# Turning picked heads on GpSimd, adding bias and sinks on TensorE, and another order where a mixer takes over

## The chip, the cores and the metric

The kernel runs on one core of one Trainium2 chip. The metric is device microseconds of one execution; less is better. Engines are called by their names: TensorE multiplies matrices (PE, and PEld for its weight loads), VectorE (DVE), ScalarE (ACT) and GpSimd (POOL) work element by element, SyncE (SP) issues DMAs.

## The reference

A decoder trunk of two layers works on 256 tokens of width 1024, everything in fp32. Each layer is a mixer and a squared-ReLU MLP, each between a modulation and a LayerNorm:

```python
for layer in range(DEPTH):
    shift, scale, gate = ada_modulation(c, ada_w[layer, 0], ada_b[layer, 0])   # silu(c) @ w + b
    h = x * (1.0 + scale) + shift
    y = mixer_ab(h, ...) if layer % 2 == 0 else mixer_c(h, ...)
    x = layer_norm(DN_ALPHA * x + gate * y, ln_g[layer, 0], ln_b[layer, 0])
    ...                                       # the same again with the MLP in place of the mixer
```

`mixer_ab` of layer 0 has two groups of eight heads. Group A attends in a window of 128 tokens, and each head has a learned sink, a logit that takes part in the softmax but has no value. Group B scores all keys with a small indexer, picks the 64 best for each query and attends to these; its queries are `apply_rope(cq @ w_uq)`, those of the indexer `apply_rope(cq @ w_uiq)`. The rotary embedding is

```python
t1, t2 = jnp.split(t, 2, axis=-1)
rot = jnp.concatenate([-t2, t1], axis=-1)
return t * cos + rot * sin
```

`mixer_c` of layer 1 has sixteen heads with rotary queries and keys and plain causal attention (there is one block of 256 keys only).

## The kernel before

The 256 tokens are two blocks b of 128, one token to a partition. Products that need fp32's precision at a higher rate are split: a weight w is copied by ScalarE to wh (line 182), VectorE subtracts to get wl (line 183, for `w_out` GpSimd does it), and `mm3` adds three fp32r products (lines 263 to 265, tiles ps_m, ps_c, ps_out). The first attention runs on plain fp32 matmuls.

A scheduler orders each engine's instructions from the program's order, priorities (`later(n)` moves a piece back) and added dependencies without a semaphore (`behind(what, m)` places m after the last instruction noted under that name). What an engine then runs is a fixed list, and an instruction that waits holds up all behind it on its engine. PSUM tiles come from four pools a to d of two buffers each: ps_ada and ps_uq are in a, ps_s (scores) and ps_i (index scores) in b, transposes (ps_T, ps_pt, ps_mod) in c, ps_pv in d.

**The first attention** (about 50 to 100 us). `b_queries` multiplies the queries of group B (which = 0) or of the indexer (1) into ps_uq (line 819), `rope` turns them on VectorE (lines 503 to 507: one product with the cosine, one half product each with the two halves of the sine, one sum), `to_T` transposes (line 523) and ScalarE copies to bqT or iqT (line 525). `iq(0)`, `iq(1)`, `bq(0)`, `bq(1)` are written before the attention, bq with a lower priority. `index` computes index scores (ps_i; relu at line 854 on ScalarE; the weighted sum at line 857 on VectorE), `select` picks eight at a time (lines 868, 869 and at the end 873).

`attend` runs four half steps for each block and group (`half_step`, a pipeline of three stages): scores on TensorE (line 564), mask and minimum on VectorE (line 568), exp on ScalarE (line 572), transposes (line 578), and products with the values into ps_pv (line 586), whose 65th column of each head is the sum. Behind every second half step VectorE forms the denominator: for group A the sink term (`sinkexp`, line 595, from negm and the constant nsink, both in SBUF; exp at line 596; line 597 adds), reciprocal (598), and the scaled output y (602).

Beside each half step `ada_rows` multiplies a piece of the conditioning weights (eight matmuls of 128x256, line 378, tile ps_ada), ScalarE copies the rows (line 389, adarows), two matmuls turn them to columns (line 400, 128x1 each), and VectorE adds the bias on the way to mods (line 409). All of these and the attention's matmuls are chained with `in_turn`, so their order on TensorE is as written. Ten such pieces lie in this stretch.

**The turn to layer 1's mixer** (about 318 to 338 us). `renew` ends MLP 0: `finish` issues the last MLP products and the residual with its statistics (lines 641 to 643), `norm` takes the moments, GpSimd's power (line 329) and normalises z (line 659), `modulate` transposes z (ps_mod, line 475), applies scale and shift (ScalarE line 480, VectorE line 483), and splits to hTh and hTl, which the products ps_c of `c_in` need. VectorE also has the wl splits of the first two pieces of `c_in` (ci_0, ci_1) to do; `firsts` lists them, and they are held behind named places: the casts and subtractions of both behind the last ul of MLP 0, and block 0's moments behind the last of the four subtractions.

Of the kernel before, what the change touches and what calls it, by code (L numbers as in the profile page):

```python
# [69 lines left out]
def trunk(ctx: ExitStack, tc, c, x, pos, small, ln, ada, w_g, w_g1, w_uq, w_out, c_in, c_out, w1, w2, out):  # L70
# [398 lines left out]
    def modulate(src, b, i, hT):  # L469

        for h in range(2):
# [13 lines left out]
            split(hT[0][:, 4 * h:4 * h + 4, b * P:(b + 1) * P], hT[1][:, 4 * h:4 * h + 4, b * P:(b + 1) * P], t)  # L485
# [10 lines left out]
    def rope(src, heads, b, dsts, eng=nc.vector):  # L496
# [4 lines left out]
        lo = sinT[:, b:b + 1, :32].to_broadcast([P, heads, 32])  # L501
        hi = sinT[:, b:b + 1, 32:].to_broadcast([P, heads, 32])
# [55 lines left out]
    def half_step(b, p0, half, qT, kT, vv, mask, y, heads, head, sinks, negm, pv):  # L558
# [32 lines left out]
        pv = pv[:, :260].rearrange("p (h j e) -> p h j e", h=2, j=2)  # L591
# [328 lines left out]
    todo = {"i": index_keys, "q": bq, "s": pick, "a": a_prep, "k": iq}  # L920
# [3 lines left out]
    ops = lambda t: steps(*[(todo[n[0]], int(n[1])) for n in t.split()])  # L924
# [72 lines left out]
    def mlp(l, hT, rest, rows):  # L997
# [86 lines left out]
        def finish(b, zst):  # L1084
# [3 lines left out]
            for h in range(2):  # L1088
# [123 lines left out]
```

## Time and profile before

| | |
|---|---|
| time, three runs | 649.32, 649.54, 651.75 us; median 649.54 |
| the profiled execution's own time, its span | 652.39 us, 650.6 us |
| TensorE busy, granted clock over the span | 627.3 us (96%), 0.987 |
| VectorE, ScalarE, GpSimd busy | 467.7 (72%), 336.7 (52%), 49.0 us (8%) |
| HBM read | 149.83 MB, 232 GB/s over the span |

The profiled execution is one execution of the program with the hardware profiler on. Its span runs from the first to the last instruction and is 1.8 us shorter than its time. A busy share is an average over stages with different limits, so stages are looked at one by one. The chain that ended last follows the work back from the last instruction, at each step to what released it. A row counts records of the profiler; line numbers are those of the kernel before.

### The profile page before, as it was taken

The numbers are of one execution on the slowest core, as the hardware profiler recorded it, in microseconds if no ns is written. First come the engines' busy times: TensorE is split into PE (matmuls) and PEld (weight loads), VectorE is DVE, ScalarE is ACT, GpSimd is POOL, SyncE is SP. The second block draws the span as 40 slices with busy tenths as digits, with TensorE's granted clock in tenths as the row PEclk, the third lists the DMA queues.
The fourth block names the chain that finished last, engine by engine and source line by source line (L and its number), as shares of the span: only waits on it lengthen the run. The fifth ranks groups of instructions, "written<-read, shape, count | busy, mean of one in ns | idle before, by whom it ended". The sixth has DMA issues, their size and how long they took to land.

```text
span 650.6 us, 9762 instructions
## 1 busy us (share of the span) xinstructions
PE 627.3 (96%) x3762; PEld 527.5 (81%) x3762; DVE 467.7 (72%) x859; ACT 336.7 (52%) x534; POOL 49.0 (8%) x73
## 2 busy tenths in 40 slices
PE   5998999999999999999989999999999999999994
PEld 3554778887989899898868888888889899998983
DVE  2948885797788889977987985845876755554447
ACT  3315668375454545446635456845564545455440
POOL 5010045200010000200001000000000000000001
PEclk8899999999999999999989999999999999999998
DMA  8999346654799978999733783501567745665101
GB/s 305 409 409 415 134 136 261 245 202 138 268 349 338 382 271 313 386 330 371 281 129 130 262 320 130 194 1 65 194 243 273 275 179 194 224 230 193 67 1 64
DMA packets 25392, 151.50 MB, mean 233 GB/s; under 512 B 2945, under 2 KB 3329, under 8 KB 10114
## 3 DMA queue, kind: packets, MB, share of 16 engines
q1 hardware_dynamic: 25058, 150.50, 63.1%
q8 instruction: 29, 0.48, 0.3%
q10 hardware_dynamic: 288, 0.39, 0.2%
q14 instruction: 17, 0.14, 0.1%
HBM read 149.83 MB, written 1.05 MB: 232 GB/s over the span
## 4 chain that ended last, share of the span: by engine, by line
PE 90%; DVE 4%; ACT 3%; DMA 1%; issue 1%; POOL 0%; SPq 0%; DVEq 0%; ACTq 0%
PE ps_m L263 18%; PE ps_m L265 18%; PE ps_m L264 18%; PE ps_c L263 4%; PE ps_c L264 4%; PE ps_c L265 3%; PE ps_g L696 3%; PE ps_s L564 3%; PE ps_pv L586 3%; PE ps_g L716 2%; PE ps_out L265 2%; PE ps_out L263 2%; PE ps_out L264 2%; PE ps_pt L578 2%; PE ps_ada L378 1%; ACT h L480 1%
## 5 line engine op out<-in xcount | busy, mean ns | idle before, releaser
L183 DVE TENSOR_TENSOR wl<-w_w,wh 128x1024 fp32r<-128x1024 f32 x128 | 153.6, 1222 | 78.0 <-ACT wh L182 77.9
L182 ACT CAST wh<-w_w 128x1024 fp32r<-128x1024 f32 x128 | 131.2, 1050 | 150.7 <-PE ps_m L264 72.8
L263 PE MATMUL ps_m<-hTh,wh 128*128 128x256 f32 x448 | 126.7, 283 | 0.0
L265 PE MATMUL ps_m<-hTh,wl 128*128 128x256 f32 x448 | 126.6, 283 | 0.0
L264 PE MATMUL ps_m<-hTl,wh 128*128 128x256 f32 x448 | 126.6, 283 | 0.0
L263 PE MATMUL ps_m<-wh,uh 128*128 128x512 f32 x256 | 101.5, 397 | 0.1
L265 PE MATMUL ps_m<-wh,ul 128*128 128x512 f32 x256 | 101.6, 397 | 0.0
L264 PE MATMUL ps_m<-wl,uh 128*128 128x512 f32 x256 | 101.0, 394 | 0.0
L349 DVE CUSTOM_DVE_ANT_0 junk<-w_ada,cB,sm 128x1024 bf16<-128x1024 f32 x72 | 92.8, 1289 | 10.0 <-DMA w_ada<-in_ada_dram 8.5
L264 PEld LDWEIGHTS ps_m<-hTl,wh 128*128 128x128 f32 x448 | 85.6, 191 | 1.3
L263 PEld LDWEIGHTS ps_m<-hTh,wh 128*128 128x128 f32 x448 | 85.6, 191 | 1.2
L265 PEld LDWEIGHTS ps_m<-hTh,wl 128*128 128x128 f32 x448 | 85.6, 191 | 0.1
L265 PEld LDWEIGHTS ps_m<-wh,ul 128*128 128x128 f32 x256 | 48.2, 188 | 11.5 <-DVE ul L183 0.4
L263 PEld LDWEIGHTS ps_m<-wh,uh 128*128 128x128 f32 x256 | 48.4, 189 | 10.2 <-ACT uh L182 0.5
L264 PEld LDWEIGHTS ps_m<-wl,uh 128*128 128x128 f32 x256 | 48.2, 188 | 9.7
L263 PE MATMUL ps_c<-wh,hTh 128*128 128x512 f32 x96 | 38.8, 407 | 2.1 <-ACT hTh L182 2.1
L264 PE MATMUL ps_c<-wl,hTh 128*128 128x512 f32 x96 | 38.8, 406 | 0.0
L265 PE MATMUL ps_c<-wh,hTl 128*128 128x512 f32 x96 | 37.8, 397 | 0.0
L329 POOL TENSOR_TENSOR rs<-rs,mhalf 128x1 f32<-128x1 f32 x8 | 8.0, 1000 | 333.0 <-DVE rs L649 333.0
L572 ACT ACTIVATE prob<-prob,negm 128x128 f32<-128x128 f32 (+1 forms) x64 | 26.6, 451 | 12.3 <-DVE negm L568 12.1
L183 DVE TENSOR_TENSOR wl<-w_ci,wh 128x1024 fp32r<-128x1024 f32 x24 | 28.8, 1221 | 5.6 <-ACT wh L182 5.6
L182 ACT CAST wh<-w_ci 128x1024 fp32r<-128x1024 f32 x24 | 24.8, 1051 | 13.7 <-PE ps_c L265 9.9
(226 smaller groups left out, 995.2 us busy)
## 6 DMA issues: line engine op xcount, KB each, us to landing
w_w<-in_w_dram SPq DMA_DIRECT2D x64, 1024.0 KB, 4.9
w_ada<-in_ada_dram SPq DMA_DIRECT2D x34, 1024.0 KB, 6.9
w_ada<-in_ada_dram SPq DMA_DIRECT2D x24, 512.0 KB, 9.5
w_ci<-in_c_in_dram SPq DMA_DIRECT2D x12, 1024.0 KB, 6.4
w_wo<-in_w_out_dram SPq DMA_DIRECT2D x4, 1024.0 KB, 7.4
w_co<-in_c_out_dram SPq DMA_DIRECT2D x4, 1024.0 KB, 5.0
w_g<-in_w_g_dram SPq DMA_DIRECT2D x8, 356.0 KB, 9.1
early<-in_ada_dram SPq DMA_DIRECT2D x4, 512.0 KB, 9.1
```

Of the source, the lines that this page charges most:

```text
L182: state["cast"] = nc.scalar.copy(dh, src)
L183: return eng.tensor_sub(dl, src, dh.bitcast(F32))
L263: return [nc.tensor.matmul(ps, a[0], b[0], start=start, stop=False), nc.tensor.matmul(ps, a[0], b[1], start=False, stop=False), nc.tensor. ...
L264: nc.tensor.matmul(ps, a[0], b[1], start=False, stop=False),
L265: nc.tensor.matmul(ps, a[1], b[0], start=False, stop=stop)]
L349: state[key, j] = nc.vector.tensor_tensor_reduce(out=junk, in0=w, in1=cB, scale=1.0, scalar=bias, op0=ALU.mult, op1=ALU.add, accum_out=m)
L564: in_turn(nc.tensor.matmul(ps[:, j * 256:j * 256 + nk], qT[:, p0 + j, b * P:(b + 1) * P], kT(p0 + j, half)[:, :nk], start=True, stop=True))
L572: state["exp"] = nc.scalar.activation(pr[:, j, :nk], pr[:, j, :nk], AF.Exp, bias=negm[:, hd:hd + 1], scale=-1.0)
L578: in_turn(nc.tensor.transpose(pt[:, o:o + P], pr[:, j, kb * P:(kb + 1) * P], ident))
L586: in_turn(nc.tensor.matmul(pv[:, i * 65:(i + 1) * 65], flat[:, o:o + P], vv(kb, head(p0 + j, half)), start=(kb == 0), stop=(kb == b)))
L696: nc.tensor.matmul(ps[b][:, :s.stop - s.start], hk[:, b * P:(b + 1) * P], w[:, s], start=k == 0, stop=k == KT - 1)
L716: nc.tensor.matmul(g1[b], hk[:, b * P:(b + 1) * P], parts["g1", k // 2][0][:, k % 2 * 512:k % 2 * 512 + 512], start=k == 0, stop=k == KT - 1)
```

## The change

Five things are changed.

1. **Queries of the picked heads (bq).** ScalarE copies ps_uq to SBUF, and GpSimd does the four rotary steps (three products, one sum). They are no longer written before the attention but within it (steps `q0`, `q1`, and for the transposes `t0`, `t1`). The transposes take their place among the matmuls in turn.
2. **The conditioning's bias.** A matmul of the identity with two columns of sm (128x2) begins the accumulation in ps_ada, the two column matmuls add to it, and ScalarE copies to mods; VectorE's addition goes.
3. **Sinks.** For group A, a matmul of nsink with the identity writes the eight sink values to columns 260 to 267 of ps_pv at the start of a half's work; line 605 subtracts from there and so reads PSUM.
4. **Rotary half products.** On VectorE the two half products become one instruction that reads the halves in reverse, here and in layer 1.
5. **The order at the turn to layer 1's mixer.** Block 0's residual is behind the first subtraction of ci_0 alone; the second one's cast goes behind the cast that was noted last before `modulate`, the subtractions of the later ones behind `modulate`'s own split; in `modulate` of layer 1 block 0, ScalarE does the first two of each four slices and VectorE the other two.

```diff
@@ ada_columns, ada_end
+        a, z, step = ada_span(key)
+        biases = sm[:, S_ADAB + 24 * key[1] + a:S_ADAB + 24 * key[1] + z:step]
+        in_turn(nc.tensor.matmul(ps[:, 256:258], ident, biases, start=True, stop=False))
         for j in range(2):
-            in_turn(nc.tensor.matmul(ps[:, 256 + j:257 + j], rows[:, j * P:(j + 1) * P], four, start=True, stop=True))
+            in_turn(nc.tensor.matmul(ps[:, 256 + j:257 + j], rows[:, j * P:(j + 1) * P], four, start=False, stop=j == 1))
...
-        behind("least", nc.vector.tensor_add(mods[i][:, a:z:step], ps[:, 256:258],
-                                             sm[:, S_ADAB + 24 * i + a:S_ADAB + 24 * i + z:step]))
+        behind("exp", nc.scalar.copy(mods[key[1]][:, a:z:step], ps[:, 256:258]))
@@ modulate
-                if (h == 0 or b == 0) and not (i == 2 and b == h == 0 and j > 1):
+                if j < 2 if i == 2 and b == 0 else h == 0 or b == 0:
...
-            split(hT[0][:, 4 * h:4 * h + 4, b * P:(b + 1) * P], hT[1][:, 4 * h:4 * h + 4, b * P:(b + 1) * P], t)
+            state["split"] = split(hT[0][:, 4 * h:4 * h + 4, b * P:(b + 1) * P],
+                                   hT[1][:, 4 * h:4 * h + 4, b * P:(b + 1) * P], t)
@@ rope
-        eng.tensor_mul(t2[:, :, :32], src[:, :, 32:], lo)
-        eng.tensor_mul(t2[:, :, 32:], src[:, :, :32], hi)
+        halves = lambda t: t.rearrange("p h (t d) -> p h t d", t=2)
+        eng.tensor_mul(halves(t2), halves(src)[:, :, ::-1, :], sn)
@@ attend, half_step
             pv = pd("ps_pv")
+            if sinks:
+                in_turn(nc.tensor.matmul(pv[:, 260:268], ident, nsink, start=True, stop=True))
...
-            nc.vector.tensor_sub(ex, *(t.rearrange(heads, h=2)[:, :, p0:p0 + 2] for t in (negm, nsink)))
+            nc.vector.tensor_sub(ex, *(t.rearrange(heads, h=2)[:, :, p0:p0 + 2] for t in (negm, sunk)))
@@ renew
             if b == 0:
-                behind("moments", firsts[-1][1])
+                behind("norm", firsts[1][1])
             ahead(1)
+            m = state["cast"]
             modulate(zs[b][0], b, i, hT)
+            if b == 0:
+                behind("cast", m)
+                for _, low in firsts[2:]:
+                    behind("split", low)
+                state["firsts"] = firsts[-1][1]
@@ the steps beside the attention
     def bq(b):
-        b_rope(b_queries(0, b), [bqT], b)
+        if not lates_q:
+            lates_q.update({n: work.tile([P, NB, 8, HD], F32, name=n, tag="q4", bufs=5) for n in ("bq", "bq1", "bq2")})
+        t, t1, t2 = (lates_q[n][:, b] for n in ("bq", "bq1", "bq2"))
+        nc.scalar.copy(t, heads_of(b_queries(0, b)))
...
+        nc.gpsimd.tensor_mul(t1, t, cs)
+        nc.gpsimd.tensor_mul(t2[:, :, :32], t[:, :, 32:], lo)
+        nc.gpsimd.tensor_mul(t2[:, :, 32:], t[:, :, :32], hi)
+        nc.gpsimd.tensor_add(t1, t1, t2)
...
-    with later(40):
-        for b in range(NB):
-            bq(b)
...
-    st = ["a0", "i0 a1 i1 s0", "a1", "s0 s0 s0 s1", "b0", "b1"]
+    st = ["a0", "i0 a1 i1+q0+q1 s0", "a1", "s0 s0+t0 s0+t1 s1", "b0", "b1"]
@@ mlp
                 for cast, low in firsts:
                     behind("cast", cast)
-                    behind("vector", low)
+                behind("vector", firsts[0][1])
...
-                behind("norm" if held and b else None if held else "done", m)
+                behind("firsts" if held and b else None if held else "done", m)
```

The order that results is shown at two places.

TensorE, before, where the first group of four heads of block 0 ends (ps_pv_560) and the first scores of block 1 are next (ps_s_757; its keys are 256, two of the matmuls make one half step):

```order
L564 MATMUL ps_s_720<-keys_395,aqT_466 128x128 x2
L578 MATMUL ps_pt_728<-ident_132,prob_663 128x128 x2
L586 MATMUL ps_pv_560<-vA_404,probT_673 128x65 x2
L400 MATMUL ps_ada_679<-four_137,adarows_718 128x1 x2
L378 MATMUL ps_ada_737<-w_ada_293,cT_130 32x256 x4
L378 MATMUL ps_ada_737<-w_ada_294,cT_130 32x256 x4
L564 MATMUL ps_s_757<-keys_395,aqT_466 128x256 x2
L578 MATMUL ps_pt_765<-ident_132,prob_721 128x128 x2
L586 MATMUL ps_pv_658<-vA_404,probT_731 128x65 x2
```

TensorE now, from the last index scores of block 1 to the same scores (here ps_s_742; ps_uq_684 and 692 are the queries of the picked heads, ps_pv_522 is the group that ends, L401 the bias, L547 the sinks of the next group in ps_pv_737):

```order
L868 MATMUL ps_i_674<-keys_395,iqT_463 128x256 x2
L835 MATMUL ps_uq_684<-w_uq_279,pair_394 128x512 x2
L574 MATMUL ps_s_703<-keys_395,aqT_464 128x128 x2
L588 MATMUL ps_pt_711<-ident_132,prob_626 128x128 x2
L835 MATMUL ps_uq_692<-w_uq_279,pair_394 128x512 x2
L596 MATMUL ps_pv_522<-vA_404,probT_636 128x65 x2
L401 MATMUL ps_ada_643<-sm_75,ident_132 128x2
L403 MATMUL ps_ada_643<-four_137,adarows_701 128x1 x2
L378 MATMUL ps_ada_721<-w_ada_293,cT_130 32x256 x4
L378 MATMUL ps_ada_721<-w_ada_294,cT_130 32x256 x4
L547 MATMUL ps_pv_737<-nsink_167,ident_132 128x8
L574 MATMUL ps_s_742<-keys_395,aqT_464 128x256 x2
```

Two query products of 2 x 128x512, the bias and the sinks stand in front of the scores now. Pool d has two buffers, so ps_pv_737 takes the one of ps_pv_522 and its sinks wait until that is read for the last time, which is VectorE's y0 at line 612. In the order before, the first matmul into ps_pv_753, the third of these tiles, stands behind the scores ps_s_837, two half steps further on.

VectorE, before, from the denominator of that group to its y0 (score_578 are the index scores of block 0, score_688 of block 1):

```order
L597 TENSOR_TENSOR den_772<-ps_pv_560,sinkexp_773 128x4
L595 TENSOR_TENSOR sinkexp_857<-negm_559,nsink_167 128x4
L868 MAX mx_884<-score_578 128x8
L568 ISA prob_758,negm_752<-ps_s_757,mA_141,nsink_167 128x256
L568 ISA negm_752 128x1
L568 ISA prob_758,negm_752<-ps_s_757,mA_141,nsink_167 128x256
L568 ISA negm_752 128x1
L598 RECIPROCAL den_772<-den_772 128x4
L409 TENSOR_TENSOR mod0_169<-ps_ada_737,sm_75 128x2
L602 TENSOR_TENSOR y0_468<-ps_pv_560,den_772 128x2x128
```

VectorE now, the rows that end with the y0 for which the sinks of ps_pv_737 wait (score_541 and score_652 are the index scores of the two blocks):

```order
L884 MAX mx_938<-score_652 128x8
L885 MATCH_REPLACE score_541<-mx_882,score_541 128x128
L885 MATCH_REPLACE score_652<-mx_938,score_652 128x256
L889 SCALAR_TENSOR_TENSOR pair_394<-mC_142,score_541 128x128
L884 MAX mx_941<-score_652 128x8
L605 TENSOR_TENSOR sinkexp_758<-negm_521,ps_pv_522 128x4
L885 MATCH_REPLACE score_652<-mx_941,score_652 128x256
L607 TENSOR_TENSOR den_757<-ps_pv_522,sinkexp_758 128x4
L884 MAX mx_993<-score_652 128x8
L608 RECIPROCAL den_757<-den_757 128x4
L885 MATCH_REPLACE score_652<-mx_993,score_652 128x256
L612 TENSOR_TENSOR y0_466<-ps_pv_522,den_757 128x2x128
```

The picks of both blocks lie between the sink's difference and y0 now, and the scores' row of the next half step (line 568 before) no longer stands ahead of y0 but behind it.

At the turn to layer 1's mixer, TensorE before, where block 0's transposes of z (ps_mod) stand among the last products of MLP 0 (ps_m_1446 is block 1's second half):

```order
L263 MATMUL ps_m_1446<-wh,uh 128x512
L264 MATMUL ps_m_1446<-wl,uh 128x512
L475 MATMUL ps_mod<-ident,z 128x128 x8
L265 MATMUL ps_m_1446<-wh,ul 128x512
L263 MATMUL ps_m_1446<-wh,uh 128x512
L264 MATMUL ps_m_1446<-wl,uh 128x512
L265 MATMUL ps_m_1446<-wh,ul 128x512
L263 MATMUL ps_c<-wh,hTh 128x512
```

TensorE now (ps_m_1450 and 1451 are the two halves of block 1; behind the last row shown come eleven more matmuls into them before the first into ps_c):

```order
L263 MATMUL ps_m_1451<-wh,uh 128x512
L481 MATMUL ps_mod<-ident,z 128x128 x8
L264 MATMUL ps_m_1451<-wl,uh 128x512
L265 MATMUL ps_m_1451<-wh,ul 128x512
L263 MATMUL ps_m_1451<-wh,uh 128x512
L264 MATMUL ps_m_1451<-wl,uh 128x512
L265 MATMUL ps_m_1451<-wh,ul 128x512
L263 MATMUL ps_m_1450<-wh,uh 128x512
```

Four matmuls lay between ps_mod and ps_c, and 17 do now.

VectorE before, from the first subtractions of ci_0 (w_ci_3124) to the normalised z:

```order
L183 TENSOR_TENSOR wl<-w_ci_3124,wh 128x1024 x2
L641 TENSOR_TENSOR z<-ps_m_1443,gateB 128x512
L641 TENSOR_TENSOR z<-ps_m_1444,gateB 128x512
L642 SCALAR_TENSOR_TENSOR z<-x_79,z 128x512 x2
L643 BN_STATS stats<-z 128x6 x2
L183 TENSOR_TENSOR wl<-w_ci_3130,wh 128x1024
L647 BN_AGGR mv<-stats 128x2
L649 TENSOR_SCALAR rs<-mv 128x1
L183 TENSOR_TENSOR wl<-w_ci_3130,wh 128x1024
L659 TENSOR_SCALAR z<-z,mv,rs 128x512 x2
```

VectorE now, the same stretch (w_ci_3129 is ci_0):

```order
L183 TENSOR_TENSOR wl<-w_ci_3129,wh 128x1024
L651 TENSOR_TENSOR z<-ps_m_1448,gateB 128x512
L652 SCALAR_TENSOR_TENSOR z<-x_79,z 128x512
L651 TENSOR_TENSOR z<-ps_m_1449,gateB 128x512
L653 BN_STATS stats<-z 128x6
L652 SCALAR_TENSOR_TENSOR z<-x_79,z 128x512
L653 BN_STATS stats<-z 128x6
L657 BN_AGGR mv<-stats 128x2
L659 TENSOR_SCALAR rs<-mv 128x1
L669 TENSOR_SCALAR z<-z,mv,rs 128x512 x2
```

Three of the four subtractions of ci_0 and ci_1 that stood ahead of z stand behind it, and the two halves of the residual follow each other in another order.

## Rows read from the trace of the kernel before

**Rows 1.** The profile's page: busy time of each engine, its share of the span and its instructions, the chain that ended last by engine, and the costliest group (count, busy us, mean ns of one, idle before it).

```profile
PE 627.3 (96%) x3762; PEld 527.5 (81%) x3762; DVE 467.7 (72%) x859; ACT 336.7 (52%) x534; POOL 49.0 (8%) x73
...
PE 90%; DVE 4%; ACT 3%; DMA 1%; issue 1%; POOL 0%; SPq 0%; DVEq 0%; ACTq 0%
...
L183 DVE TENSOR_TENSOR wl<-w_w,wh 128x1024 fp32r<-128x1024 f32 x128 | 153.6, 1222 | 78.0 <-ACT wh L182 77.9
```

**Rows 2.** Busy time by stage. Columns: the stretch, its length, then busy time and instructions of PE, PEld, DVE, ACT and POOL, the granted clock of TensorE, the DMA share and GB/s.

```profile
50.00:72.00 22.00, 18.69 (x122) 11.51 (x121) 19.48 (x66) 12.89 (x39) 0.00 (x0) 1.00 0.95 383
72.00:95.00 23.00, 23.00 (x220) 18.19 (x218) 19.26 (x85) 13.81 (x33) 5.67 (x7) 1.00 0.19 55
95.00:130.00 35.00, 34.55 (x238) 28.29 (x237) 22.35 (x77) 22.04 (x44) 15.00 (x7) 1.00 0.71 261
...
345.00:475.00 130.00, 129.10 (x732) 108.86 (x731) 97.15 (x201) 78.91 (x137) 2.97 (x3) 1.00 0.46 163
```

**Rows 3.** What TensorE waited for between 50 and 165 us: the waiting line, the work it waited for, us in total, times, longest.

```profile
PE ps_T L523 <- DVE qr L507: 1.4, 2, 1.1
PE ps_uq L819 <- ACT pair L781: 1.1, 1, 1.1
...
PE ps_s L564 <- ACT aqT L525: 0.8, 1, 0.8
```

**Rows 4.** The chain that ended last, in the first attention: start us, us, what. A row counts records; one fp32 matmul leaves two, a transpose one.

```profile
57.85 0.86 PE ps_uq L819 x2
...
77.33 0.22 PE ps_pt L578 x2
77.54 0.39 PE ps_pv L586 x4
77.94 0.39 PE ps_ada L400 x4
78.33 1.00 PE ps_ada L378 x16
79.33 1.06 PE ps_s L564 x4
```

**Rows 5.** VectorE's instructions between 50 and 130 us by line and shape: count, busy us, mean ns of one, idle before them.

```profile
L507 DVE TENSOR_TENSOR qr<-rope,rope 128x512 f32<-128x512 f32 x6 | 4.1, 688 | 0.1
L868 DVE MAX8 mx<-score 128x8 f32<-128x256 f32 x8 | 3.4, 420 | 0.1
L602 DVE TENSOR_TENSOR y<-ps_pv,den 128x256 f32<-128x256 f32 x8 | 3.3, 416 | 0.1
L869 DVE MATCH_REPLACE8 score<-mx,score 128x256 f32<-128x256 f32 x8 | 3.3, 408 | 0.0
L503 DVE TENSOR_TENSOR rope<-ps_uq,cosT 128x512 f32<-128x512 f32 x4 | 2.7, 686 | 0.0
L568 DVE CUSTOM_DVE_ANT_0 prob<-ps_s,mA,nsink 128x128 f32<-128x128 f32 x8 | 2.7, 346 | 0.0
L504 DVE TENSOR_TENSOR rope<-ps_uq,sinT 128x256 f32<-128x256 f32 x4 | 1.7, 416 | 0.0
L409 DVE TENSOR_TENSOR mod<-ps_ada,sm 128x2 f32<-128x2 f32 x10 | 1.6, 157 | 3.2 <-PE ps_ada L400 1.7 <-ACT prob L572 1.2
L597 DVE TENSOR_TENSOR den<-ps_pv,sinkexp 128x4 f32<-128x4 f32 x4 | 0.6, 153 | 0.0
```

**Rows 6.** The same view for ScalarE and GpSimd.

```profile
L854 ACT ACTIVATE rl<-ps_i 128x512 f32<-128x512 f32 x4 | 2.4, 597 | 1.4 <-PE ps_i L852 1.4
L525 ACT COPY bqT<-ps_T 128x512 f32<-128x512 f32 x2 | 1.2, 586 | 2.1 <-PE ps_T L523 2.1
...
L183 POOL TENSOR_TENSOR wl<-w_wo,wh 128x1024 fp32r<-128x1024 f32 x6 | 14.1, 2372 | 8.4 <-ACT wh L182 8.4
```

**Rows 7.** The timeline of GpSimd and of VectorE around 93 us: start us, us, engine, line, operation.

```profile
90.00 4.69 POOL L183 TENSOR_TENSOR hTl<-w_wo,hTh 128x1024 fp32r<-128x1024 f32 x2 [6.29 <-ACT hTh L182]
...
92.81 1.90 DVE L595 TENSOR_TENSOR sinkexp<-negm,nsink 128x4 f32<-128x4 f32 x1
```

**Rows 8.** The forms of the instruction at line 595: minimum, median and maximum ns.

```profile
L595 DVE TENSOR_TENSOR sinkexp<-negm,nsink x4: 144/154/1899, 71.6 to 92.8; 128x4 f32<-128x4 f32 x4
```

**Rows 9.** The end of MLP 0 and the start of layer 1 on VectorE: start us, us, what.

```profile
318.17 1.28 DVE L641 TENSOR_TENSOR z<-ps_m,gateB 128x512 f32<-128x512 f32 x2
319.37 1.29 DVE L642 SCALAR_TENSOR_TENSOR z<-x,z 128x512 f32<-128x512 f32 x2
...
324.86 1.00 DVE L659 TENSOR_SCALAR z<-z,mv,rs 128x512 f32<-128x512 f32 x2 [0.44 <-POOL rs L329]
```

**Rows 10.** The chain that ended last over the same stretch: start us, us, what.

```profile
325.87 0.45 PE ps_mod L475 x4
...
329.78 0.50 PE ps_c L263
...
330.98 0.43 PE ps_c L264
...
334.15 0.24 PE ps_c L263
```

**Rows 11.** What TensorE waited for between 310 and 350 us, and the granted clock of 330 to 340 us.

```profile
PE ps_c L263 <- ACT hTh L182: 2.1, 1, 2.1
...
330.00:340.00 10.00, 10.00 (x42) 8.13 (x42) 8.06 (x16) 2.36 (x6) 0.55 (x1) 0.83 0.31 105
```

More of the change, by code (lines that the diff above doesn't have):

```diff
@@ L500, in rope @@
         cs = cosT[:, b:b + 1, :].to_broadcast([P, heads, HD])
-        lo = sinT[:, b:b + 1, :32].to_broadcast([P, heads, 32])
-        hi = sinT[:, b:b + 1, 32:].to_broadcast([P, heads, 32])
+        sn = sinT[:, b:b + 1, :].to_broadcast([P, heads, HD]).rearrange("p h (t d) -> p h t d", t=2)
         eng.tensor_mul(t1, src, cs)
-        eng.tensor_mul(t2[:, :, :32], src[:, :, 32:], lo)
-        eng.tensor_mul(t2[:, :, 32:], src[:, :, :32], hi)
+        halves = lambda t: t.rearrange("p h (t d) -> p h t d", t=2)
+        eng.tensor_mul(halves(t2), halves(src)[:, :, ::-1, :], sn)
         for d, view in dsts:
@@ L517, in heads_of, with to_T @@
         return t.rearrange("p (h d) -> p h d", d=HD)
-    def to_T(srcs, dst):
+    def to_T(srcs, dst, turn=False):
         ps = pc("ps_T")
         for j, s in enumerate(srcs):
-            nc.tensor.transpose(ps[:, j * P:(j + 1) * P], s, ident)
+            m = nc.tensor.transpose(ps[:, j * P:(j + 1) * P], s, ident)
+            if turn:
+                behind("turn", m)
         for d, rows in dst:
@@ L590, in half_step @@
             return
-        pv = pv[:, :260].rearrange("p (h j e) -> p h j e", h=2, j=2)
+        pv, sunk = pv[:, :260].rearrange("p (h j e) -> p h j e", h=2, j=2), pv[:, 260:268]
         den = col([P, 2, 2, 1], "den")
@@ L803, in q4, with to_qT @@
         return work.tile([P, 4, 256], F32, name=name, tag="q4", bufs=5)
-    def to_qT(qf, dst, b):
+    def to_qT(qf, dst, b, turn=False):
         n = P // len(dst)
         to_T([qf[:, j * P:(j + 1) * P] for j in range(4)],
-             [(d[:, :, b * P:(b + 1) * P], slice(i * n, (i + 1) * n)) for i, d in enumerate(dst)])
+             [(d[:, :, b * P:(b + 1) * P], slice(i * n, (i + 1) * n)) for i, d in enumerate(dst)], turn)
     iqT, aqT = q4("iqT"), q4("aqT")
@@ L894, in steps @@
     def steps(*todo):
-        for f, *args in todo:
-            with later(LATER.get(names[f] + str(args[0]), 0)):
-                f(*args)
+        for group in todo:
+            for f, *args in group:
+                with later(LATER.get(names[f] + str(args[0]), 0)):
+                    f(*args)
             yield
@@ L901, in iq, with bq_T @@
         b_rope(b_queries(1, b), [iqT], b)
+    lates_q = {}
     def bq(b):
-        b_rope(b_queries(0, b), [bqT], b)
+        if not lates_q:
+            lates_q.update({n: work.tile([P, NB, 8, HD], F32, name=n, tag="q4", bufs=5) for n in ("bq", "bq1", "bq2")})
+        t, t1, t2 = (lates_q[n][:, b] for n in ("bq", "bq1", "bq2"))
+        nc.scalar.copy(t, heads_of(b_queries(0, b)))
+        cs = cosT[:, b:b + 1, :].to_broadcast([P, 8, HD])
+        lo = sinT[:, b:b + 1, :32].to_broadcast([P, 8, 32])
+        hi = sinT[:, b:b + 1, 32:].to_broadcast([P, 8, 32])
+        nc.gpsimd.tensor_mul(t1, t, cs)
+        nc.gpsimd.tensor_mul(t2[:, :, :32], t[:, :, 32:], lo)
+        nc.gpsimd.tensor_mul(t2[:, :, 32:], t[:, :, :32], hi)
+        nc.gpsimd.tensor_add(t1, t1, t2)
+    def bq_T(b):
+        t = lates_q["bq1"][:, b].rearrange("p h d -> p (h d)")
+        to_qT(t, [bqT], b, True)
     a_prep(0)
@@ L918, in pick @@
         next(picks[b], None)
-    todo = {"i": index_keys, "q": bq, "s": pick, "a": a_prep, "k": iq}
+    todo = {"i": index_keys, "q": bq, "s": pick, "a": a_prep, "k": iq, "t": bq_T}
     names = {f: n for n, f in todo.items()}
-    st = ["a0", "i0 a1 i1 s0", "a1", "s0 s0 s0 s1", "b0", "b1"]
+    st = ["a0", "i0 a1 i1+q0+q1 s0", "a1", "s0 s0+t0 s0+t1 s1", "b0", "b1"]
     side = lambda n: (a_side if n[0] == "a" else b_side)(int(n[1]))
-    ops = lambda t: steps(*[(todo[n[0]], int(n[1])) for n in t.split()])
+    ops = lambda t: steps(*[[(todo[n[0]], int(n[1])) for n in g.split("+")] for g in t.split()])
     together(side(st[0]), ops(st[1]))
```

6 lines of the change are left out of this document (4 added, 2 removed).

## The prediction

> **What bounds the kernel now.** I read the page first: TensorE is busy 627.3 of 650.6 us and 90% of the chain that ended last lies on it [rows 1]. So a change counts by what it adds to or takes from TensorE's row of work, and by the waits that it opens or closes there. The windows by stage show where there is room. From 50 to 72 us TensorE is busy 18.69 of 22, so 3.3 us are idle; from 72 to 95 it is busy 23.00 of 23, and from 345 to 475 129.10 of 130 [rows 2]. The list of its waits names three of the idle times in the first stretch: 1.4 us for the turned queries qr of VectorE, 1.1 for ScalarE's pair, 0.8 for aqT [rows 3]. The other hole of interest is at the turn to layer 1: 2.1 us before the first ps_c, for hTh [rows 11], and matmuls of 0.43 us behind it that take 0.23 to 0.24 later [rows 10], at a granted clock of 0.83 for 330 to 340 us [rows 11].
>
> **Matmuls added.** Ten biases (128x2) and four sinks (128x8) go to TensorE. The trace has neither form. Two column matmuls of 128x1 take 0.39 us and two of 128x65 (ps_pv) 0.39 [rows 4], so both widths that enclose the new ones cost 0.195, and I take 0.20. The lowest price would be that of a transpose, two in 0.22 [rows 4], or 0.11. The first sink falls into the idle time before the queries; 13 x 0.20 = **2.6 us** (1.4 to 2.6). They stand in line with a TensorE that has no idle time there [rows 2], so nothing hides them. VectorE gives up ten additions of 0.157 [rows 5], which saves nothing where it is not waited for.
>
> **The queries of the picked heads.** TensorE's part is only moved: four matmuls of 0.86 [rows 4] and eight transposes go from the stretch with idle time into the one without. VectorE gives up two ropes of 0.69 + 0.42 + 0.42 + 0.69 = 2.2 us [rows 5], and the waits for qr, **1.4 us** [rows 3], should close (0 to 1.4). But what these matmuls covered is now bare: the index scores follow each other directly, through two PSUM buffers that ScalarE empties at 0.60 us a pair of wide ones [rows 6], and ScalarE has two more copies of 0.59 [rows 6] between them. I put **1.5 us** of new waits for ScalarE there, 1.0 before the scores of block 1 and 0.5 before those of block 0. None would be possible if ScalarE is always ahead; 3.2 if it falls behind at each of six places by about one relu.
>
> GpSimd needs 2.37 us for 128x1024 [rows 6], so by estimate 1.19 for 128x512 and 0.59 for 128x256: 3.6 us a block, 7.1 for both, and from 50 to 72 us it did nothing before [rows 2]. From a block's query product to its transposes lie over two half steps, of 0.22 + 0.39 + 0.39 + 1.00 + 1.06 = 3.06 us each [rows 4], against 0.59 for the copy and 3.6: 0, and a wait of about 1 only if GpSimd takes twice as long.
>
> Its instructions can also hold up VectorE. While GpSimd ran two instructions from 90.00 to 94.69, line 595 took 1.90 us [rows 7], where the median is 0.154 [rows 8]: 1.75 lost once. Line 595 now reads PSUM, but line 857 adds two operands from SBUF, and its last rows fall beside the new GpSimd work. Bounds 0 and 3; I take **0.3 us**, for most of it would meet a VectorE that is ahead. The Trainium skill ("SBUF — State Buffer", section "SBUF: two separate sides") says that GpSimd and VectorE share a pair of ports as an exclusive lock, which an instruction of VectorE with two SBUF inputs needs too, and that the loser waits for the whole instruction. By that the row above is the rule and not an accident, and the sum would be that of the rival on GpSimd below instead of the one here.
>
> **The sinks' wait.** A new wait, as the order shows: the sinks of the third ps_pv need VectorE's y0 of the first, and behind them on TensorE stand the scores of block 1 and all the rest. Counted from the end of the last scores of block 0, TensorE needs 0.22 (transposes) + 0.86 (queries) + 0.39 (ps_pv) + 0.20 (bias) + 0.39 (columns) + 1.00 (conditioning) = 3.06 us to the sinks [rows 4]. VectorE has by the order two score rows of 0.35, three picks of block 0 priced like them (1.04), three times 0.42 and three times 0.41 for block 1, then 0.15 three times (difference, denominator, reciprocal) and 0.416 [rows 5, 8]: 5.1 us. Instructions in a row overlap: two of 0.69 start at 318.17 and the next at 319.37 [rows 5, 9], 0.60 apart, so 0.09 is saved on each, and the 15 need some 4.0. The wait is 4.0 - 3.06 = 0.9 to 5.1 - 3.06 = 2.0; I take **1.7**, since VectorE also comes late to these scores, with four weighted sums of the index still ahead. The sinks of the fourth ps_pv wait for the second y0 in the same way, with 0.44 of transposes more before them: **0.9 us** (0 to 1.35). In the trace of before nothing of the kind is waited for, because ps_pv is first written two half steps later.
>
> **One half product instead of two.** VectorE saves at most 2 x 0.416 - 0.69 = 0.14 us a rope [rows 5]. In layer 1 TensorE has no more than 0.9 us idle in 130 [rows 2], so 0.
>
> **Later in the attention** 0.45 us are idle from 95 to 130 [rows 2]; a later TensorE finds more things ready: -0.3 (0 to -0.45).
>
> **The turn to layer 1.** The hole costs 2.1 us, and seven matmuls at 0.43 instead of 0.23 another 1.4 [rows 10, 11]: 3.5 us. Now two subtractions of about 1.2 [rows 1] fewer precede z, so z is ready 2.3 us earlier than 324.86 [rows 9]. TensorE comes to ps_mod 13 x 0.23 = 3.0 us earlier than 325.87 [rows 10]; with half of z still to write it waits some 0.9 us. Behind ps_mod come 17 matmuls, 3.9 us, instead of four, and hT (3.9 us from ps_mod to ps_c in the chain of before, less with ScalarE and VectorE at half the slices each) is then ready in time, so the hole and the slow matmuls go. But VectorE is busy 8.06 of 10 us behind it already [rows 11], and three subtractions (3.6 us) that were done before now fall among the products: I put 1.9 us of waits for late wl at two or three places. New loss 2.8, gain **0.7 us** (2.6 gained to 1.0 lost).
>
> **Sum.** 2.6 + 1.5 + 0.3 + 1.7 + 0.9 - 1.4 - 0.3 - 0.7 = +4.6 us. On the profiled execution (652.39) that is 657.0; this one lies 2.85 above the median, and from the median of 649.54 it gives **654.1 us**. A difference of 0.5%, 3.2 us, is about what a measurement can tell from none: 646.3 to 652.8 is "same".
>
> **Rivals.** *VectorE is ahead everywhere.* With two ropes less it may reach y0 earlier than I count: sinks' waits 0.5 together, ScalarE's 0.5, GpSimd's 0. Then 2.6 + 0.5 + 0.5 - 1.4 - 0.3 - 0.7 = +1.2, 650.7 us. For it: 4.4 us of VectorE's 19.48 between 50 and 72 go [rows 2, 5]. Against it: picks are moved ahead of y0.
>
> *Faster: the hole at the turn closes in full.* If the late wl come in time and z before TensorE gets to ps_mod, all 3.5 us are gained. With no new waits in the attention and the additions at 2.0 (half way to the price of a transpose), 2.0 - 1.4 - 0.4 - 3.5 = -3.3, 646.2 us. It decides whether VectorE's idle 1.9 us of 330 to 340 [rows 11] and what TensorE's 17 matmuls give it are enough for the 3.6 moved there; that they must nearly fit to the piece speaks against it.
>
> *GpSimd holds VectorE.* Two losses like the 1.75 of line 595, scaled to instructions of half the length, and their delay passed to y0 and the sinks: +2.5 on the forecast, 656.6 us. For it: the one long instruction [rows 7, 8]. Against it: GpSimd's sum of one block is over before most of the picks, whose inputs are a single tensor. This is what the rule of the Trainium skill, "SBUF — State Buffer", "SBUF: two separate sides", asks for.
>
> *The clock falls behind the sinks' wait.* After 2.1 us of idle at the turn seven matmuls ran at the clock's lower level, 1.2 instead of 2.4 GHz [rows 10, 11]; the waits of 1.1 us between 50 and 72 left it at 1.00 [rows 2, 3]. A wait of 1.7 lies between. If it falls, 1.4 us more: 655.5.
>
> **How the numbers follow.** Forecast 0.40, VectorE ahead 0.27, faster 0.13, GpSimd's hold 0.12, clock 0.08. The forecast and the last two are slower by over 0.5%: 0.60. The second is the same, 0.27, the third faster, 0.13. The range reaches from 647.0 to 657.5: at the lower end it leaves out the faster case for the most part, at the upper what is beyond both of the costlier ones, together no more than 2 in 10. The likeliest case alone runs from 652.5 to 656.
>
> **What would show it.** Right: TensorE idle before the third and fourth sinks (line 547), named for VectorE's y; ten matmuls at line 401 of 0.2 us; no wait of ps_T for qr; waits for ScalarE's rl before ps_i; at the turn a wait of ps_mod for z of about 1 us, none of ps_c for hTh of 2 us, a clock of 1.00 in 330 to 340, and small waits of ps_c for wl. Wrong: sinks without a wait, or TensorE idle before the transposes of bq for GpSimd, or a turn to layer 1 that still has 2 us of idle time in one piece.

## The result and the profile after

The changed kernel takes 654.95 us (median of 5 runs, 654.15 to 657.4), the kernel before 649.35 (5 runs beside it, 649.1 to 651.75): a ratio of 1.0074 over the runs, 95% interval 1.0055 to 1.0092, or 4.8 us. The quotient of the two medians is 1.0086 (5.6 us); the times of the kernel before gather near 649.3 and near 651.4 us, so a median of few runs moves by up to 2 us, and the ratio with its interval is the figure to go by. The forecast was 654.1 us and slower, by 4.6 us, so sign and size are right; two of its terms were too small, as shown below.

The page of the changed kernel, with the line that answers to [rows 1], and the chain by engine:

```profile
PE 629.9 (96%) x3790; PEld 529.1 (81%) x3790; DVE 461.3 (71%) x827; ACT 337.7 (52%) x544; POOL 57.0 (9%) x81
...
PE 90%; DVE 5%; ACT 3%; issue 1%; POOL 0%; DMA 0%; DVEq 0%; ACTq 0%
```

Its windows by stage, columns as in [rows 2], with the one of the turn to layer 1:

```profile
50.00:72.00 22.00, 20.16 (x144) 13.68 (x144) 18.21 (x63) 13.01 (x40) 0.00 (x0) 1.00 0.78 316
72.00:95.00 23.00, 20.98 (x172) 15.50 (x170) 16.10 (x71) 11.95 (x30) 10.65 (x14) 1.00 0.22 76
95.00:130.00 35.00, 35.00 (x269) 29.38 (x269) 18.73 (x64) 24.19 (x54) 17.78 (x9) 1.00 0.71 267
...
312.00:345.00 33.00, 32.14 (x167) 26.19 (x166) 30.20 (x48) 16.71 (x25) 1.10 (x2) 1.00 0.60 221
```

TensorE's idle time from 50 to 72 us fell from 3.3 to 1.8 us, the 0.45 from 95 to 130 went, but from 72 to 95, where there was none, 2.0 us are idle now. What TensorE waited for between 45 and 165 us (columns as in [rows 3]; L574 is the scores, L868 the index scores, L519 the copy of ps_g that frees a PSUM buffer):

```profile
PE ps_pv L547 <- DVE y L612: 2.0, 2, 1.2
...
PE ps_s L574 <- ACT aqT L533: 0.8, 1, 0.8
PE ps_i L868 <- ACT rl L870: 0.7, 1, 0.7
PE ps_pv L547 <- ACT evac L519: 0.6, 1, 0.6
```

The waits for qr are gone, and the sinks wait 2.0 us for y in two pieces. Both stand in the chain that ended last (columns as in [rows 4]); L401 is the bias, L403 the columns, L547 the sinks, L612 y, and L574, L588 and L835 at the head the last scores of block 0, their transposes and the second query product:

```profile
74.39 0.45 PE ps_s L574 x4
74.84 0.22 PE ps_pt L588 x2
...
75.07 1.98 PE ps_uq L835 x4
77.05 0.39 PE ps_pv L596 x4
77.44 0.17 PE ps_ada L401 x2
77.61 0.46 PE ps_ada L403 x4
...
79.41 0.34 DVE y L612
...
79.89 0.36 PE ps_pv L547 x2
80.25 0.97 PE ps_s L574 x4
...
88.15 0.43 DVE y L612
...
88.72 0.36 PE ps_pv L547 x2
```

The new matmuls by form: count, minimum, median and maximum ns, first and last start, shapes (two records to a matmul):

```profile
L401 PE MATMUL ps_ada<-sm,ident x20: 170/237/251, 62.5 to 105.9; 128*128 128x2 f32 x20
...
L547 PE MATMUL ps_pv<-nsink,ident x8: 175/252/256, 49.8 to 88.8; 128*128 128x8 f32 x8
```

A record is 0.17 to 0.25 us long, but records overlap: in the chain a bias takes 0.17 us, and the two columns behind it 0.45 where they took 0.39 [rows 4]. Ten biases are 2.3 us.

GpSimd's timeline for the first block's queries:

```profile
75.09 1.28 POOL L931 TENSOR_TENSOR bq<-bq,cosT 128x512 f32<-128x512 f32 x1 [27.01 <-ACT bq L927]
76.33 0.72 POOL L932 TENSOR_TENSOR bq<-bq,sinT 128x256 f32<-128x256 f32 x1
77.01 0.77 POOL L933 TENSOR_TENSOR bq<-bq,sinT 128x256 f32<-128x256 f32 x1
77.86 1.28 POOL L934 TENSOR_TENSOR bq<-bq,bq 128x512 f32<-128x512 f32 x1
```

At the turn to layer 1 the chain comes to ps_mod (L481) with no idle time before it, and the only wait up to 350 us is one for wl; the last line is the window of 330 to 340 us with the granted clock of 1.00, where [rows 11] has 0.83:

```profile
326.98 0.23 PE ps_m L263
327.22 0.07 issue
327.29 0.64 PE ps_mod L481 x4
```

```profile
PE ps_c L264 <- DVE wl L183: 0.6, 1, 0.6
```

```profile
330.00:340.00 10.00, 9.36 (x42) 7.32 (x41) 9.87 (x15) 2.77 (x4) 0.00 (x0) 1.00 0.54 197
```

Where the time lies between two executions is read from when the same work starts on TensorE:

| TensorE starts | before | after | added in the stage |
|---|---|---|---|
| first ps_uq | 51.4 | 50.3 | -1.1 |
| ps_bt, the gate behind the attention | 107.8 | 112.4 | +5.7 |
| first ps_c | 329.8 | 332.1 | -2.3 |
| last ps_c | 408.4 | 410.9 | +0.2 |
| end of the span | 650.6 | 653.0 | -0.1 |

So the first attention costs 5.7 us and the turn gives 2.3 back, 3.5 us from the first ps_uq to the end. The 1.1 us ahead of the first ps_uq are not the change's: of what was changed only the first sinks matmul, at 49.84 us, lies there, and in the traces of the fourteen kernels of this document the first ps_uq starts anywhere between 49.0 and 51.4 us (the granted clock from 10 to 20 us was 0.66 in the one execution and 0.83 in the other). The profiled execution of before took 652.39 us, 3.0 above the median of 649.35; so the spans differ by 2.4 us and the medians by 5.6.

### The profile page after: what moved, and what is told of

It reads as the page before. It is cut to its first block, busy times and chain, and to the rows that moved or that the text cites. A ratio compares the mean times of both kernels' runs of the same rounds, so it can differ in the third digit from the quotient of the medians.

```text
span 653.0 us, 9804 instructions
## 1 busy us (share of the span) xinstructions
PE 629.9 (96%) x3790; PEld 529.1 (81%) x3790; DVE 461.3 (71%) x827; ACT 337.7 (52%) x544; POOL 57.0 (9%) x81
## 4 chain that ended last, share of the span: by engine, by line
PE 90%; DVE 5%; ACT 3%; issue 1%; POOL 0%; DMA 0%; DVEq 0%; ACTq 0%
PE ps_m L263 18%; PE ps_m L265 18%; PE ps_m L264 18%; PE ps_s L574 3%; PE ps_g L712 3%; PE ps_c L263 3%; PE ps_c L264 3%; PE ps_c L265 3%; PE ps_pv L596 3%; PE ps_g L732 2%; PE ps_out L263 2%; PE ps_out L265 2%; PE ps_out L264 2%; PE ps_pt L588 2%; PE ps_T L529 2%; PE ps_ada L378 1%
```

## Experiments

Each was timed beside the kernel before, which had medians of 650.63 (runs e1 to e4), 650.23 (e5 to e8) and 651.22 us (e9 to e12), so the ratios are to be compared, not the times; 0.001 is 0.65 us. The last two columns are read from the one trace of each kernel, as in the table above: "attention" from the first ps_uq to ps_bt, "to layer 1" from ps_bt to the first ps_c, in us. They leave out the start, which varies, but they show one execution only.

| run | what it is | us | ratio, interval | attention | to layer 1 |
|---|---|---|---|---|---|
| | the kernel before | 649.35 | 1 | 56.4 | 222.0 |
| | the change | 654.95 | 1.0074 (1.0055 to 1.0092) | 62.1 | 219.7 |
| e1 | the change without sinks in PSUM | 652.56 | 1.0029 (1.0017 to 1.0041) | 61.8 | 219.9 |
| e2 | the change without the bias on TensorE | 652.73 | 1.0046 (1.0027 to 1.0065) | 59.7 | 219.6 |
| e3 | the change with the queries on VectorE | 659.69 | 1.0138 (1.0109 to 1.0167) | 68.0 | 219.6 |
| e4 | the change with the old turn | 657.19 | 1.0104 (1.0086 to 1.0121) | 62.1 | 221.8 |
| e5 | the change, sinks one half step later | 652.72 | 1.0039 (1.0026 to 1.0053) | 60.9 | 219.8 |
| e6 | before, with sinks in PSUM | 657.85 | 1.0119 (1.0099 to 1.0139) | 62.8 | 221.6 |
| e7 | before, with new turn and half products | 649.77 | 0.9990 (0.9975 to 1.0004) | 56.5 | 220.0 |
| e8 | e7 with the queries on GpSimd | 649.02 | 0.9981 (0.9970 to 0.9992) | 56.3 | 220.0 |
| e9 | before, with half products | 651.91 | 1.0013 (1.0000 to 1.0026) | 56.4 | 221.9 |
| e10 | before, with the new turn | 649.20 | 0.9974 (0.9963 to 0.9986) | 56.5 | 219.9 |
| e11 | before, with the bias on TensorE | 652.48 | 1.0024 (1.0011 to 1.0036) | 58.5 | 221.9 |
| e12 | e10 with the queries on GpSimd | 649.37 | 0.9977 (0.9966 to 0.9988) | 56.9 | 219.9 |

### The sinks (e1, e5, e6)

e1 takes them back to SBUF:

```diff
-            if sinks:
-                in_turn(nc.tensor.matmul(pv[:, 260:268], ident, nsink, start=True, stop=True))
...
-            nc.vector.tensor_sub(ex, *(t.rearrange(heads, h=2)[:, :, p0:p0 + 2] for t in (negm, sunk)))
+            nc.vector.tensor_sub(ex, *(t.rearrange(heads, h=2)[:, :, p0:p0 + 2] for t in (negm, nsink)))
```

> The changed kernel with the sinks taken from SBUF again, all else as changed. Theory (added matmuls and new waits on TensorE's row add up): three sinks matmuls of about 0.2 us in line and the two waits for VectorE's y (0.83 and 1.18 us in the changed kernel's trace) go, 2.6 us: 652.3 us from 654.95. Rival (the queries of the picked heads cost the time; the sinks' waits only stand where another wait for VectorE would stand): the waits come back as waits of ps_s or ps_pt a half step later, at most 0.6 us gained, 654.4 us.

1.0029 against 1.0074: 2.9 us gained, the theory's 2.6. No wait for VectorE came back in the attention, but TensorE, being earlier, now waits for a load of conditioning weights. The wait, and a window behind it (columns as before):

```profile
PE ps_ada L378 <- DMA w_ada<-in_ada_dram: 1.0, 1, 1.0
```

```profile
102.00:103.00 1.00, 1.00 (x6) 1.00 (x6) 0.11 (x1) 0.13 (x1) 0.00 (x0) 0.50 1.04 426
...
104.00:105.00 1.00, 1.00 (x7) 1.00 (x7) 0.00 (x0) 1.00 (x3) 0.00 (x0) 0.50 1.02 426
105.00:106.00 1.00, 1.00 (x9) 1.00 (x10) 0.00 (x0) 0.79 (x3) 0.00 (x0) 1.00 1.02 426
```

From 102 to 105 us the granted clock is 0.50, the lower of its two levels (1.2 of 2.4 GHz), behind an idle time of 1.04 us; the prediction's rival had it fall behind some 2 us. In this trace, of an execution that took 653.77 us where e1's median is 652.56, the load's wait and the low clock take nearly all of the gain back: 61.8 us of attention against 62.1.

e5 keeps the matmuls and moves them in front of the first product into ps_pv:

```diff
         yield
+        if sinks and half == 0:
+            in_turn(nc.tensor.matmul(pv[:, 260:268], ident, nsink, start=True, stop=True))
         for j in range(2):
```

> The changed kernel with the four sinks matmuls kept, but placed in front of the first product with the values into ps_pv, one half step later. Theory (the buffer's wait is the larger part of what the sinks cost): the two waits for y, 2.0 us, go and the matmuls stay: 652.9 us from 654.95, a little more if the w_ada load, which was waited for 1.0 us without the sinks, is late here too. Rival (the matmuls in line are the cost, the wait only moves to the place where TensorE needs the buffer): 654.5 to 655 us, with the same waits at the new place.

1.0039: 2.3 us gained (1.2 in the attention of its trace). Of the waits in its trace none is the sinks', and the load is waited for here too:

```profile
PE ps_uq L835 <- ACT pair L797: 1.1, 1, 1.1
...
PE ps_ada L378 <- DMA w_ada<-in_ada_dram: 0.8, 1, 0.8
PE ps_s L572 <- ACT aqT L533: 0.8, 1, 0.8
```

So the wait is the larger part of what the sinks cost, and it does not move to the new place, where y has long been written: the first group's y0 ends at 79.47 us in this trace, and the sinks of the third ps_pv stand at 87.54.

e6 puts the two places of e1's diff into the kernel before.

> The kernel before with the sinks in PSUM alone. Theory (VectorE's lateness sets the wait, and the queries of the picked heads on VectorE make it later): waits for y of about 4 us together as in the run with those queries back on VectorE, 0.6 us of matmuls, and the lower clock behind a wait of 2 us in some executions: 653.5 to 657 us. Rival (the wait came from the moved queries and the picks moved ahead of y): at most 1.5 us of waits, 651 to 652 us.

1.0119, 7.7 us, a little above the theory's upper end and far from the rival. Its waits for y (L604) are double those of the changed kernel, 2.04 and 2.06 us; behind the first the granted clock stayed at 1.00, behind the second it fell:

```profile
PE ps_pv L539 <- DVE y L604: 4.1, 2, 2.1
```

```profile
90.00:92.00 2.00, 2.00 (x10) 1.80 (x9) 1.24 (x5) 0.42 (x1) 0.00 (x0) 0.50 0.00 0
```

### The queries (e3, e8, e12)

e3 undoes the move. e8 leaves out sinks and bias, so it is e7 with the move, and e12 also the half products, so it is e10 with it.

```diff
     def bq(b):
...
+        b_rope(b_queries(0, b), [bqT], b)
...
+    with later(40):
+        for b in range(NB):
+            bq(b)
...
-    st = ["a0", "i0 a1 i1+q0+q1 s0", "a1", "s0 s0+t0 s0+t1 s1", "b0", "b1"]
+    st = ["a0", "i0 a1 i1 s0", "a1", "s0 s0 s0 s1", "b0", "b1"]
```

> The changed kernel with the queries of the picked heads written before the attention and turned by VectorE again, all else as changed. Theory: the moved queries cost nothing by themselves, the time that TensorE loses beside them (0.7 us for ScalarE's relu) is about what the waits for qr cost before (1.4 us): 654 to 656 us. Rival: they are the larger part of the 5.6 us, because four matmuls of 0.86 us no longer cover the waits between 50 and 72 us: 651 to 652 us.

1.0138 instead of 1.0074: 4.2 us lost (5.9 in the attention of its trace), where theory expected nothing and the rival a gain. Both were wrong. TensorE's waits and three windows behind the second wait show why:

```profile
PE ps_pv L547 <- DVE y L612: 4.0, 2, 2.1
PE ps_T L529 <- DVE qr L513: 1.9, 2, 1.6
```

```profile
92.00:96.00 4.00, 4.00 (x20) 3.80 (x18) 1.24 (x5) 1.39 (x3) 0.00 (x0) 0.50 0.00 0
96.00:100.00 4.00, 4.00 (x23) 2.24 (x23) 0.00 (x0) 2.42 (x4) 2.52 (x2) 0.50 0.18 31
100.00:104.00 4.00, 4.00 (x44) 3.40 (x43) 1.35 (x8) 2.38 (x7) 2.14 (x1) 1.00 0.57 236
```

With two ropes more on VectorE its y0 comes later, the sinks wait 4.0 us instead of 2.0 (1.94 and 2.06), and behind the second wait, which ends at 90.15 us, the granted clock is 0.50 for about ten us; behind the first it stayed at 1.00. The queries' move had been paying for the sinks.

> The changed kernel without sinks in PSUM and without the bias on TensorE: queries of the picked heads on GpSimd, half products and the new turn. Theory (the two single gains of 2.9 and 1.8 us add): 650.2 us, ratio 1.000, or up to 1 us more where the w_ada load is waited for longer. Rival (moving the queries is a gain of its own of some 4 us, as undoing it in the changed kernel lost 4.2): ratio 0.991, 644 us.

0.9981: 1.3 us better than the sum of the two single gains, which is within the noise of the four measurements, and far from the rival's 0.991. Without the sinks the queries' move is worth next to nothing: e8 is 0.6 us faster than e7, and the intervals overlap.

> The kernel before with the queries of the picked heads on GpSimd and the new turn; no sinks in PSUM, no bias on TensorE, half products in two steps. Theory: as with the half products (ratio 0.998), since VectorE is ahead here and its 0.14 us a rope are not waited for: 0.9975 to 0.9985. Rival (the queries' move costs what the lost cover costs, and the half products paid for it): 1.000 or more.

0.9977, against 0.9974 of e10, which differs by the queries alone: 0.2 us, no difference clear of noise. From the first ps_uq to ps_bt e12 takes 56.9 us and e10 56.5.

### The bias (e2, e11)

```diff
-        in_turn(nc.tensor.matmul(ps[:, 256:258], ident, biases, start=True, stop=False))
...
-        behind("exp", nc.scalar.copy(mods[key[1]][:, a:z:step], ps[:, 256:258]))
+        behind("least", nc.vector.tensor_add(mods[i][:, a:z:step], ps[:, 256:258],
+                                             sm[:, S_ADAB + 24 * i + a:S_ADAB + 24 * i + z:step]))
```

> The changed kernel with the conditioning's bias added by VectorE again, all else as changed. Theory: ten matmuls of 128x2 of 0.17 to 0.23 us leave TensorE's row, 2.0 us: 652.9 us. Rival: VectorE's ten additions of 0.16 us come back in front of y0, the sinks wait longer by most of it, and nothing is gained: 654.5 to 655.0 us.

> The kernel before with the conditioning's bias on TensorE alone. Theory: ten matmuls in line, each 0.17 us and 0.06 more for the column matmuls behind it, 2.3 us: ratio 1.0035, 651.8 to 652.5 us. Rival (VectorE, which is freed of ten additions, gives it back): ratio 0.999 to 1.001.

Undone 1.8 us are gained, alone 1.6 are lost (0.7 to 2.3): matmuls in line, as in the theories, at 0.16 to 0.18 us each; in the attention of the traces it is 2.4 and 2.1 us, nearer to the 2.3 expected. Undone, the rival's mechanism is there too and takes part of the gain, for the sinks (L546 there) wait 2.7 us instead of 2.0:

```profile
PE ps_pv L546 <- DVE y L611: 2.7, 2, 1.5
```

### The turn and the half products (e4, e7, e9, e10)

The edit of e4 is the change's diff in `modulate`, `renew` and `mlp` in reverse, as for example

```diff
-                behind("norm", firsts[1][1])
+                behind("moments", firsts[-1][1])
```

That of e10 is the same forward on the kernel before, that of e9 the change's diff in `rope`, and e7 has both.

> The changed kernel with the old order at the turn to layer 1's mixer, all else as changed. Theory: the hole of 2.1 us before the first ps_c comes back, and the 0.64 us wait for wl goes; with the slow matmuls behind the hole 2.0 us or more are lost, without them 1.4: 656.4 to 657.0 us. Rival (the hole is paid for later, or was not there in most executions): 654.3 to 655.3 us.

1.0104: 2.0 us lost. The hole of 2.1 us is back, but not the slow matmuls: the clock stayed at 1.00. TensorE's waits from 326 us on, and its first 5 us of ps_c:

```profile
PE ps_c L263 <- ACT hTh L182: 2.1, 1, 2.1
PE ps_T L528 <- DVE qr L512: 1.2, 1, 1.2
```

```profile
334.50:339.50 5.00, 5.00 (x22) 4.10 (x23) 4.54 (x8) 0.00 (x0) 0.31 (x1) 1.00 0.19 25
```

The same 5 us in e9, whose hole is also 2.1 us and whose clock fell:

```profile
329.00:334.00 5.00, 4.95 (x15) 3.93 (x16) 4.59 (x8) 0.00 (x0) 0.23 (x1) 0.66 0.21 26
```

15 matmuls instead of 22, and yet the first and the last ps_c of e9 are 78.8 us apart and those of e4 78.7. At full clock TensorE waits 1.2 us for VectorE's qr at 380 us, at the low clock it has no such wait. So in these two traces the slow matmuls cost nothing by the end of ps_c.

> The kernel before with the new order at the turn to layer 1's mixer alone. Theory (the hole of 2.1 us goes, a wait of 0.64 us comes, the slow matmuls behind the hole are in few executions): 1.5 us gained, ratio 0.9975 to 0.998. Rival (the gain belongs to the changed kernel and its later start): 0.999 to 1.001.

0.9974 (1.7 us gained): the theory. In the column "to layer 1" all kernels with the new turn, e10 among them, have 219.6 to 220.0 us and all with the old one 221.6 to 222.0, whatever else they change. [rows 11]'s wait for hTh is gone and this one is there:

```profile
PE ps_c L264 <- DVE wl L183: 0.6, 1, 0.6
```

> The kernel before with the new order at the turn to layer 1's mixer and the one-step half products, nothing else. Theory: the turn gains 2.0 us here as it lost 2.0 when undone in the changed kernel, the half products 0 to 0.3: ratio 0.9965, 647.3 to 648 us beside 649.5. Rival (the gain at the turn belongs to the later start of the changed kernel): ratio 0.999 to 1.001.

0.9990, a smaller gain than e10's 0.9974, though the intervals overlap. The half products are what differs:

> The kernel before with the one-step half products alone. Theory: VectorE's list of the first attention comes out in another order, the wait of ps_T for qr grows (2.1 us in the run with the turn, 1.4 before), and nothing else changes: ratio 1.000 to 1.002. Rival (each of sixteen ropes gives back 0.14 us somewhere on the path): ratio 0.997 to 0.998.

1.0013 (0 to 1.7 us lost), in the theory's range: the list of VectorE comes out in another order, and TensorE waits 2.5 us for the ropes where it waited 2.2 for qr and aqT [rows 3]:

```profile
PE ps_T L522 <- DVE qr L506: 2.1, 1, 2.1
...
PE ps_uq L818 <- DVE rope L504: 0.4, 1, 0.4
```

e7 against e10 and e9 against before agree in the ratios, about 0.9 us lost, each at the edge of the noise. The traces do not show a loss: the attention takes 56.4 us in e9 and before and 56.5 in e7 and e10, and from the first ps_uq to the end of the span e9 takes 599.3 us, the kernel before 599.2. So the 0.3 us of longer waits is made up within the attention, and that the half products cost anything is not shown.

**The best.** e10, e12 and e8 beat both kernels, by 0.19 to 0.26% against before and about 0.95% against the change, and cannot be told apart. The smallest edit is e10, the new turn alone.

## Why the prediction was right, and where it was not

**Matmuls added (2.6 us) and the sinks' waits (1.7 + 0.9): the mechanism right, the sum a little small.** The bias costs 1.6 to 1.8 us, the sinks' matmuls 0.6 (e5 against e1), their waits 0.83 and 1.18 in the trace and 2.3 by e5. (The 0.6 is not clear of noise as a ratio; in line a sinks matmul takes 0.22 us, from 79.89 to the start of the next matmul at 80.11.) Together, from e8 to the change, both parts cost 0.0093 or 6.0 us, where 5.2 were forecast and the singles undone give 4.7: each undone alone opens a wait that the other had covered (the load in e1, 0.7 us more for y in e2); the 1.3 us between the two sums are within the noise. The first wait was too large in the forecast, 1.7 where 0.83 came, by a slip in TensorE's row: between the scores and the sinks I counted one matmul of 0.86 for the queries, but a query product is two of them (TensorE's order has x2). The chain shows 1.98 us for it, and 4.2 us instead of 3.06 from the end of the scores at 74.84 to the sinks' place at 79.06. VectorE was about as late as taken: y0 ends at 79.75, 4.9 us behind the scores, where 3.06 + 1.7 = 4.8 were assumed. (5.1 us less 15 times 0.09 is 3.75 and not 4.0; with both put right the forecast's own bounds would have been 0 to 1.2.) And I did not see how far this wait hangs on VectorE's load: both together are 4.1 us with the picked heads' ropes on VectorE (e6).

**The queries (-1.4 + 1.5 + 0.3): the sum right without the sinks.** +0.4 forecast, +0.2 (e12 against e10) and -0.6 (e8 against e7) measured, neither clear of noise. Beside the sinks the move is worth 4.2 us (e3), a link between the two terms that the sum does not have. The waits for qr went; of ScalarE's 1.5 us one wait of 0.7 is named. The rest did not come as waits: in e12 TensorE is busy 1.0 us longer in the attention than in e10 (55.2 against 54.2 us) and idle 0.6 less, and why it is busy longer is open. GpSimd's price, estimated at 1.19 and 0.59, was 1.28 and 0.72 to 0.77, and it was early: the first block's sum ends at 79.1 us, its transposes start at 86.9.

**GpSimd's hold (0.3, rival 0.12): not seen on the path.** It exists. The timelines of GpSimd and VectorE show the sink's difference while GpSimd runs its two subtractions, in e1, where it reads SBUF twice, and then in the change, where one input is PSUM:

```profile
89.17 4.69 POOL L183 TENSOR_TENSOR hTl<-w_wo,hTh 128x1024 fp32r<-128x1024 f32 x2 [6.01 <-ACT hTh L182]
...
91.86 2.02 DVE L603 TENSOR_TENSOR sinkexp<-negm,nsink 128x4 f32<-128x4 f32 x1
```

```profile
93.16 4.68 POOL L183 TENSOR_TENSOR hTl<-w_wo,hTh 128x1024 fp32r<-128x1024 f32 x2 [8.71 <-ACT hTh L182]
...
95.71 0.16 DVE L605 TENSOR_TENSOR sinkexp<-negm,ps_pv 128x4 f32<-128x4 f32 x1 [0.38 <-PE ps_pv L596]
```

With both inputs in SBUF it takes 2.02 us and ends with GpSimd's running instruction, at 93.9 us; with one in PSUM 0.16. It is so in every trace: 1.56 to 2.02 us in the eight kernels that read SBUF there, 0.16 in the six that read PSUM. So the sinks' move to PSUM takes VectorE out of GpSimd's way. By the rule of the Trainium skill, "SBUF — State Buffer", section "SBUF: two separate sides", only an instruction with two SBUF inputs (or in a mode that uses both ports) is held, and the trace agrees: 2.02 against 0.16 us. TensorE waited for neither.

**One half product (0): right, as far as is known.** Alone the ratio has a loss of 0 to 1.7 us, which the traces do not show; where the queries have moved, e8 against e12, there is none.

**Later in the attention (-0.3): right**, 0.45.

**The turn (-0.7): the failing step.** Measured -1.7 alone and -2.0 undone. I made the hole too dear (3.5 us, where e4 and e9 show that without the 1.4 of slow matmuls a wait of 1.2 for qr takes their place) and the new waits much too dear (2.8, where 0.64 was measured). No wait of 0.9 for z came, for TensorE and z reach ps_mod together at 327.2 us, and three late subtractions fell into time that VectorE had: from 330 to 340 us it is busy 9.87 of 10 now, and was 8.06 [rows 11].

**The clock (rival, 0.08): the case did not come, but it can.** Behind the waits of 0.83 and 1.18 the granted clock stayed at 1.00; in e3 and e6 it fell to 0.50 behind one of 2.06, and stayed at 1.00 behind those of 1.94 and 2.04 that came before.

So the sum came out within 1 us because two terms were too small by about as much, in opposite directions: 0.8 us of cost in sinks and bias, 1.0 of gain at the turn. That they cancel is luck; the sign and the order of size are not.

## What to carry to other kernels

An instruction put early on a busy in-order engine brings along the wait for the buffer that it writes, and everything behind it waits too: look who reads that buffer last, and place it where the buffer is needed anyway (e5). Parts of a change do not add: the singles here sum to 8.7 us (7.7 + 1.6 + 0.9 + 0.2 - 1.7), the whole is 4.8, because one part lightened the engine for which another waited. And a slow stretch on the busiest engine is only worth what the next wait does not give back.

## What was not expected of the hardware

The clock's fall does not go by the length of the last idle time alone: behind 2.09 us it fell in e9 (0.66 on the mean of the next 5 us) and behind 2.10 in e4 it stayed at 1.00; in e6 it stayed behind 2.04 us and fell behind 2.06, and in e1 it fell behind 1.04. What else it depends on is open; no run here varies it.
